# The second layer's modulation inside the first layer's channel mixing: VectorE multiply-adds on half slabs in a buffer of their own, in place of TensorE products on whole slabs

## The chip, the core and the metric

The kernel runs on one core of a Trainium2 chip. The metric is the device time of one execution in microseconds (us). TensorE is written PE (its weight loads PEld), VectorE DVE, ScalarE ACT, GpSimd POOL, and SyncE SP; SP issues every DMA that the text speaks of. All five take their instructions in order.

## The reference

A trunk of two layers over 512 latent tokens and 256 context tokens, 1024 channels, float32. What matters here, cut down:

```python
for i in range(DEPTH):                                   # DEPTH = 2
    mx = (silu_c @ w_ada[i] + b_ada[i])[:, None, :]      # latent:  (1024) @ (1024, 6144)
    mc = silu_cc @ w_ada[i] + b_ada[i]                   # context: the same weights
    sx1, ax1, gx1, sx2, ax2, gx2 = jnp.split(mx, 6, axis=-1)
    sc1, ac1, gc1, sc2, ac2, gc2 = jnp.split(mc, 6, axis=-1)
    ...
    x = x + gx1 * y_x
    x = x + gx2 * sqrelu_mlp(modulate(rmsnorm(x, norm2_g[i]), sx2, ax2), w_mlp1[i], w_mlp2[i])
    ...
def sqrelu_mlp(h, w1, w2):
    return jnp.square(jax.nn.relu(h @ w1)) @ w2          # 1024 -> 4096 -> 1024
```

Token mixing (convolution and attention) makes `y_x`; the context `h_ctx` goes the same way with `gc1`, `sc2`, `ac2` and `gc2`. The modulation `silu(c) @ w_ada[i]` has only two rows (latent and context), but reads 24 MB of weights per layer. It depends on no token, so layer 1's can be computed at any time before layer 1.

## The kernel before

**Layout and precision.** Channels lie on the 128 partitions, tokens in the columns: `X` is 128 x 8 x 768. Every large product keeps float32 precision in three matmuls: weights and activations are split into a high part (`whi`, `hh`, `fh`) and the remainder (`wlo`, `hl`, `fl`), and `mm3` (L102) adds high x high, high x low (L105) and low x high (L106). `fm_block` (L108) does this over the eight groups of 128 input channels: a block of 24 matmuls gives 128 output channels for one group of tokens, `LAT` (512) or `CTXS` (256).

**Weights.** `load_slab` (L84) loads 256 output columns (1 MB) into a raw buffer (tag `raw`; two of them in the channel mixing), ScalarE writes the high part in two halves (L76), and another engine the remainder (L77): VectorE, GpSimd, or one half on each (`both`). The split tiles have two buffers each in `wpool`.

**Channel mixing** (L1142 on). Four chunks `cch` of 1024 hidden channels. A chunk has two stages: four slabs of `w_mlp1`, whose blocks `f` end in `hidden` (L1144), and four slabs of `w_mlp2`, whose blocks `r` end in `residual` (L1079), which adds gate x product to `X` on VectorE. A slab has two blocks of 512 tokens (m = 0, 1), then two of 256. `hidden` does relu on ScalarE (`fr`), its square to the high part `fh` on ScalarE, the square in full precision on GpSimd in place (L1151), and the remainder `fl` on VectorE (L1152). A product lies in one of two PSUM banks for 512 tokens and one of two for 256 until relu or residual has read it. Chunk 0 of layer 0 and the second half of chunk 3 work in three groups of 256 tokens, since a norm stands ahead of the one and behind the other.

**Modulation.** `ada_slab` (L209) does 256 of the 6144 columns: a whole slab of `w_ada` (1 MB) into the same raw buffers, eight float32 products on TensorE with `cvec` (the two silu vectors) as the stationary side (L216), a copy on ScalarE (L222), two transposes on TensorE (L225) and small VectorE sums into `ad` (L228, L231). Layer 1's 24 slabs are done in layer 0's channel mixing: one behind each slab of `w_mlp1` (L1167) and one behind each slab of `w_mlp2` (L1192), so that chunks 0 to 2 hold them all.

**The norm** (`norm_mod`, L260) sums squares by matmuls with ones (`nc_n`), takes the power -1/2 on GpSimd (`ms_n`, L250), spreads it on VectorE over two diagonal tiles (`dg_n`, L253), broadcasts it by one matmul (`nb_n`, L257), and forms `nu_n`, `h2h` and `h2l` on VectorE, ScalarE and GpSimd.

**Order.** A scheduler in the framework orders each engine's instructions by a simulated timeline: program order where nothing is gained, earlier where the data are there earlier.

Of the kernel before, what the change touches and what calls it, by code (L numbers as in the profile page):

```python
# [51 lines left out]
def trunk_kernel(  # L52
# [156 lines left out]
    def ada_slab(i, L, s):  # L209
# [17 lines left out]
        for q in range(2):  # L227
# [6 lines left out]
            .to_broadcast([P, 2, 2]),  # L234
            op=ALU.add)

    def ada_gain(L, which, ks=slice(0, KT)):
# [149 lines left out]
    for i in range(DEPTH):  # L387
# [706 lines left out]

        def out_slabs(load, hidden, gate, nm, norm=None, after=None, ahead=()):
# [40 lines left out]
        if not last:  # L1136
            Ln = layer_params(i + 1)
            acc = xp.tile([P, NT], F32, tag="acc", name=f"acc{i}_3")
            ada_todo = list(range(24))
            hh = hpool.tile([P, KT, NT], F32R, tag="hh", name=f"h1h_{i + 1}")  # L1140
            hl = hpool.tile([P, KT, NT], F32R, tag="hl", name=f"h1l_{i + 1}")
        for cch in range(4):  # L1142
            fh, fl = [None] * KT, [None] * KT
            def hidden(w, mb, m, g):  # L1144
# [5 lines left out]
                nc.scalar.activation(out=fh[mb][:, g], in_=r[:, :W], func=AF.Square)  # L1150
                nc.gpsimd.tensor_tensor(out=r[:, :W], in0=r[:, :W], in1=r[:, :W], op=ALU.mult)  # L1151
                nc.vector.tensor_tensor(out=fl[mb][:, g], in0=r[:, :W], in1=f32(fh[mb][:, g]),  # L1152
# [5 lines left out]
            for s0 in ((0, 2), (2, 3), (3, 4)) if cch == 0 else ((n, n + 1) for n in range(4)):  # L1158
# [32 lines left out]
            def after(s):  # L1191
                if not last and ada_todo:  # L1192
                    ada_slab(i + 1, Ln, ada_todo.pop(0))
                if fin and not last:
                    nc.sync.dma_start(xs_d[i + 1][:, 2 * s : 2 * s + 2, :],
                                      X[:, 2 * s : 2 * s + 2, :])
                if fin and last:
# [15 lines left out]
                    w_mlp2[i][1024 * cch : 1024 * cch + 1024, 256 * s : 256 * s + 256]  # L1213
                    .rearrange("(k p) n -> p k n", p=P), f"w2_{i}_{cch}_{s}", lo_eng=None if last else both),
                lambda k: (fh[k], fl[k]), gate2, f"r{i}_{cch}",
                norm1 if fin and not last else None, after,
                (lambda: first.update(w=qk_slab(i + 1, 0, nc.gpsimd)),
                 lambda: first.update(v=v_slab(i + 1, 0, nc.gpsimd))) if fin and not last else ())
        if not last:
            while ada_todo:  # L1220
                ada_slab(i + 1, Ln, ada_todo.pop(0))
            state["ada_done"] = True
# [79 lines left out]
```

## Time and profile before

| | us |
|---|---|
| median of 3 runs | 2394.25 |
| lowest, highest run | 2392.32, 2401.45 |
| the profiled execution: its time | 2399.05 |
| the profiled execution: its span | 2397.3 |
| first `f` block of layer 0 starts at | 828.8 |
| first and last modulation products of layer 1 start near | 857.6, 1273 |
| granted TensorE clock, mean | 0.988 |

The profile is of one execution; times in it count from the start of the span. A row of the timeline gives start, duration, engine, line, operation, output<-input and shape; in brackets is the engine's idle time ahead of it and what ended that. Matmuls are pipelined, so the duration of one is longer than the step to the next. Names leave out buffer numbers: `r`, `f` and `adaps` are PSUM tiles, `r_w` a raw weight slab, `h_w` and `l_w` its two parts.

### The profile page before, as it was taken

The numbers are of one execution on the slowest core, as the hardware profiler recorded it, in microseconds if no ns is written. First come the engines' busy times: TensorE is split into PE (matmuls) and PEld (weight loads), VectorE is DVE, ScalarE is ACT, GpSimd is POOL, SyncE is SP. The second block draws the span as 40 slices with busy tenths as digits, with TensorE's granted clock in tenths as the row PEclk, the third lists the DMA queues.
The fourth block names the chain that finished last, engine by engine and source line by source line (L and its number), as shares of the span: only waits on it lengthen the run. The fifth ranks groups of instructions, "written<-read, shape, count | busy, mean of one in ns | idle before, by whom it ended". The sixth has DMA issues, their size and how long they took to land.

```text
span 2397.3 us, 36929 instructions
## 1 busy us (share of the span) xinstructions
PE 2317.9 (97%) x15034; PEld 2060.9 (86%) x15034; DVE 1349.1 (56%) x2311; ACT 928.7 (39%) x1837; POOL 679.7 (28%) x854
## 2 busy tenths in 40 slices
PE   7999999999999999999999998999999989999998
PEld 6999998888888988888888997999877879888887
DVE  6777776699556542222222356676759966433332
ACT  5555654522333342221312345555642323422331
POOL 2866754200000222120211256676620000200110
PEclk9999999999999999999999999999999999999999
DMA  8211111144535223333333221111123324232322
GB/s 292 66 43 37 45 45 42 45 158 139 163 113 176 71 89 106 124 123 106 124 114 98 78 64 54 45 43 41 47 73 132 117 72 134 82 100 90 103 90 69
DMA packets 222186, 224.79 MB, mean 94 GB/s; under 512 B 5872, under 2 KB 212160, under 8 KB 221888
## 3 DMA queue, kind: packets, MB, share of 16 engines
q1 hardware_dynamic: 222016, 222.43, 28.9%
q8 instruction: 118, 1.93, 0.3%
q14 instruction: 52, 0.43, 0.1%
HBM read 208.73 MB, written 13.67 MB: 93 GB/s over the span
## 4 chain that ended last, share of the span: by engine, by line
PE 86%; DVE 7%; ACT 3%; POOL 2%; DMA 1%; issue 1%; SPq 0%; ACTq 0%; POOLq 0%; DVEq 0%
PE r L104 6%; PE r L106 6%; PE f L104 6%; PE r L105 6%; PE f L105 6%; PE f L106 6%; PE gt L104 3%; PE gt L106 3%; PE gt L105 3%; PE qk L104 3%; PE qk L105 2%; PE qk L106 2%; PE adaps L216 2%; PE v L104 2%; PE yc L113 2%; PE v L106 2%
## 5 line engine op out<-in xcount | busy, mean ns | idle before, releaser
L104 PE MATMUL r<-fh,h_w 128*128 128x512 f32 (+1 forms) x832 | 285.8, 345 | 0.5 <-DVE X L1082 0.5
L104 PE MATMUL f<-h2h,h_w 128*128 128x512 f32 (+1 forms) x832 | 284.6, 345 | 1.3 <-ACT h2h L76 1.0
L105 PE MATMUL f<-h2l,h_w 128*128 128x512 f32 (+1 forms) x832 | 284.5, 343 | 1.1 <-POOL h2l L77 1.0
L105 PE MATMUL r<-fl,h_w 128*128 128x512 f32 (+1 forms) x832 | 283.5, 341 | 0.0
L106 PE MATMUL r<-fh,l_w 128*128 128x512 f32 (+1 forms) x832 | 283.5, 341 | 0.0
L106 PE MATMUL f<-h2h,l_w 128*128 128x512 f32 (+1 forms) x832 | 282.6, 342 | 0.0
L76 ACT ACTIVATE h_w<-r_w 128x1024 fp32r<-128x1024 f32 x128 | 128.7, 1052 | 312.1 <-PE r L105 131.0
L1151 POOL TENSOR_TENSOR fr<-fr 128x512 f32<-128x512 f32 (+1 forms) x104 | 93.1, 897 | 508.7 <-ACT fh L1150 508.7
L897 DVE SCALAR_TENSOR_TENSOR cacc<-z,cols,cacc 128x783 f32<-128x783 f32 (+1 forms) x240 | 201.2, 890 | 0.3
L104 PE MATMUL qk<-h_wqk,h1h 128*128 128x256 f32 x640 | 183.9, 289 | 5.3 <-ACT h1h L76 3.6
L1082 DVE SCALAR_TENSOR_TENSOR X<-r,ad,X 128x512 f32<-128x512 f32 (+1 forms) x104 | 64.9, 627 | 209.8 <-PE r L106 209.7
L105 PE MATMUL qk<-l_wqk,h1h 128*128 128x256 f32 x640 | 181.2, 285 | 0.0
L104 PEld LDWEIGHTS f<-h2h,h_w 128*128 128x128 f32 x832 | 157.6, 191 | 24.8 <-ACT fh L1150 2.5
L104 PEld LDWEIGHTS r<-fh,h_w 128*128 128x128 f32 x832 | 157.8, 190 | 23.6 <-issue 3.7
L106 PE MATMUL qk<-h_wqk,h1l 128*128 128x256 f32 x640 | 177.6, 285 | 0.0
L105 PEld LDWEIGHTS f<-h2l,h_w 128*128 128x128 f32 x832 | 158.4, 191 | 20.5 <-POOL h2l L77 2.5
L106 PEld LDWEIGHTS f<-h2h,l_w 128*128 128x128 f32 x832 | 158.3, 191 | 17.6
L664 DVE TENSOR_REDUCE st<-S 128x1 f32<-128x768 f32 (+1 forms) x160 | 134.7, 846 | 68.4 <-PE S L662 67.4
L106 PEld LDWEIGHTS r<-fh,l_w 128*128 128x128 f32 x832 | 157.8, 190 | 17.8
L105 PEld LDWEIGHTS r<-fl,h_w 128*128 128x128 f32 x832 | 158.0, 190 | 16.9
L77 DVE TENSOR_TENSOR l_w<-r_w,h_w 128x1024 fp32r<-128x1024 f32 x106 | 126.2, 1223 | 80.5 <-ACT h_w L76 78.9
L1152 DVE TENSOR_TENSOR fl<-fr,fh 128x512 fp32r<-128x512 f32 (+1 forms) x104 | 62.5, 605 | 189.4 <-POOL fr L1151 189.3
(247 smaller groups left out, 6257.1 us busy)
## 6 DMA issues: line engine op xcount, KB each, us to landing
r_w<-in_w_mlp_dram SPq DMA_DIRECT2D x64, 1024.0 KB, 5.4
ada<-in_w_ada_dram SPq DMA_DIRECT2D x48, 1024.0 KB, 5.2
r_wqk<-in_w_in_dram SPq DMA_DIRECT2D x32, 512.0 KB, 5.2
r_wg<-in_w_in_dram SPq DMA_DIRECT2D x16, 1024.0 KB, 5.2
r_wv<-in_w_in_dram SPq DMA_DIRECT2D x8, 1024.0 KB, 5.2
r_wao<-in_w_attn_out_dram SPq DMA_DIRECT2D x8, 1024.0 KB, 5.2
r_wo<-in_w_out_dram SPq DMA_DIRECT2D x8, 1024.0 KB, 8.2
at_d<-uo SPq DMA_DIRECT2D x40, 128.0 KB, 1.7
```

The costliest lines, as they stand in the source:

```text
L76: nc.scalar.activation(out=hi, in_=src, func=AF.Copy)
L77: (lo_eng or nc.vector).tensor_tensor(out=lo, in0=src, in1=f32(hi), op=ALU.subtract)
L104: nc.tensor.matmul(ps, sh, mh, start=first, stop=False)
L105: nc.tensor.matmul(ps, sh, ml, start=False, stop=False)
L106: nc.tensor.matmul(ps, sl, mh, start=False, stop=last)
L113: nc.tensor.matmul(ps, w[j][:, k, m0 : m0 + P], a(k)[0][:, toks], start=k + j == 0, stop=False)
L216: nc.tensor.matmul(ps[32 * j : 32 * j + 32, :256], cvec[:, k, :], r[:, k, :], start=k < 4, stop=k >= 4, tile_position=(0, 32 * j))
L664: nc.vector.tensor_reduce(out=st[:, m : m + 1], in_=S[:, :nkey], axis=AX.X, op=ALU.max, negate=True)
L897: nc.vector.scalar_tensor_tensor(out=ca[cc][:, :CV], in0=zt[cc][:, t : t + CV], scalar=wcol, in1=ca[cc][:, :CV], op0=ALU.mult, op1=ALU.add)
L1082: nc.vector.scalar_tensor_tensor(out=X[:, mb, g], in0=ps[:, :W], scalar=gate[:, s, mb : mb + 1], in1=X[:, mb, g], op0=ALU.mult, op1=ALU.add)
L1151: nc.gpsimd.tensor_tensor(out=r[:, :W], in0=r[:, :W], in1=r[:, :W], op=ALU.mult)
L1152: nc.vector.tensor_tensor(out=fl[mb][:, g], in0=r[:, :W], in1=f32(fh[mb][:, g]), op=ALU.subtract)
```

## The change

Layer 1's modulation in layer 0's channel mixing no longer uses TensorE for the product. A new generator `ada_rows` loads half a slab at a time (128 x 4 x 256, 512 KB) into a buffer `araw` of its own, of which there is one. For each of the four channel groups in the half and for each of the two rows it adds weights x a column of `cvec` into a tile `a` of 128 x 512: the first product of a slab by ScalarE, the others by VectorE's `scalar_tensor_tensor`. Then it starts the next half's load. Behind each second half, at the next step, four transposes and one reduction sum over the partitions. A step of the generator comes behind each block of 512 tokens (`tick`, `ada_step`), except the last of each `f` stage and the blocks in groups of 256: 3 + 8 steps in chunk 0, 15 in chunks 1 and 2, 7 in chunk 3, 48 in all; `drain` ends it ahead of the norm.

Two more things change. The remainders of all weight slabs in layer 0's channel mixing are made by GpSimd (before: VectorE, except three mlp1 slabs, and a half of each mlp2 slab). The full-precision square in `hidden` is made by ScalarE, in both layers.

```diff
+    def ada_rows(i, L):
+        def load(n):
+            r = state["rp"].tile([P, KT // 2, 256], F32, tag="araw", bufs=1, name=f"ar{i}_{n}")
+            nc.sync.dma_start(r, rows(w_ada[i], 256 * (n // 2), 256)[:, 4 * (n % 2) : 4 * (n % 2) + 4])
+            return r
+        r = load(0)
+        for n in range(48):
+            s = n // 2
+            if n % 2 == 0:
+                a = state["tp"].tile([P, 512], F32, tag="t2k", bufs=state["nt"], name=f"adaac{i}_{s}")
+                a = a.rearrange("p (q n) -> p q n", q=2)
+            for j in range(4):
+                k = 4 * (n % 2) + j
+                for q in range(2):
+                    if k == 0:
+                        nc.scalar.activation(out=a[:, q], in_=r[:, j], func=AF.Copy,
+                                             scale=cvec[:, k, q : q + 1])
+                    else:
+                        nc.vector.scalar_tensor_tensor(
+                            out=a[:, q], in0=r[:, j], scalar=cvec[:, k, q : q + 1], in1=a[:, q],
+                            op0=ALU.mult, op1=ALU.add)
+            if n < 47:
+                r = load(n + 1)
+            yield
+            if n % 2:
+                ps = state["mi"](f"adaps{i}_{s}")
+                for m in range(4):
+                    nc.tensor.transpose(ps[:, m * P : m * P + P],
+                                        a[:, m // 2, m % 2 * P : m % 2 * P + P], ident)
+                ad = L["ad"][:, :, 2 * s : 2 * s + 2]
+                nc.vector.tensor_reduce(out=ad, in_=ps.rearrange("p (q m k) -> p q m k", q=2, m=2),
+                                        axis=AX.X, op=ALU.add)
...
@@ out_slabs
                         out_block(w, s, g, m, hidden, gate, nm, norm)
+                        if tick and g is LAT:
+                            tick()
@@ mlp1_slab
-                                   f"w1_{i}_{cch}_{s}", lo_eng=nc.gpsimd if not last and cch + s < 2 else None)
+                                   f"w1_{i}_{cch}_{s}", lo_eng=None if last else nc.gpsimd)
@@ hidden
-                nc.gpsimd.tensor_tensor(out=r[:, :W], in0=r[:, :W], in1=r[:, :W], op=ALU.mult)
+                nc.scalar.activation(out=r[:, :W], in_=r[:, :W], func=AF.Square)
@@ the f stage
                             hidden(ws[s], 2 * s + m, m, g)
-                if not last and ada_todo:
-                    for _ in range(*s0):
-                        ada_slab(i + 1, Ln, ada_todo.pop(0))
+                            if g is LAT and (s, m) != (3, 1):
+                                ada_step()
             fin = cch == 3
             if fin and not last:
+                drain(ada_todo)
                 ada_gain(Ln, 0)
@@ after
-                if not last and ada_todo:
-                    ada_slab(i + 1, Ln, ada_todo.pop(0))
@@ the r stage
-                    .rearrange("(k p) n -> p k n", p=P), f"w2_{i}_{cch}_{s}", lo_eng=None if last else both),
+                    .rearrange("(k p) n -> p k n", p=P), f"w2_{i}_{cch}_{s}", lo_eng=None if last else nc.gpsimd),
-                norm1 if fin and not last else None, after,
+                norm1 if fin and not last else None, after, tick=ada_step, ahead=
```

How the order moves, at three places. The first is TensorE in the `r` stage of chunk 1 (names: `r_chunk_block_firsttoken`, the last number is a running one). Before, where the second slab's blocks begin:

```order
L104 MATMUL r_1_1_512_11286<-fh_1_7_10614,h_w_0_1_0_11202 128x256
L105 MATMUL r_1_1_512_11286<-fl_1_7_10615,h_w_0_1_0_11202 128x256
L106 MATMUL r_1_1_512_11286<-fh_1_7_10614,l_w_0_1_0_11203 128x256
L216 MATMUL adaps_12_11314<-ada_12_11312,cvec 32x256 x8
L104 MATMUL r_1_2_0_11338<-fh_1_0_10600,h_w_0_1_1_11332 128x512
L105 MATMUL r_1_2_0_11338<-fl_1_0_10601,h_w_0_1_1_11332 128x512
```

After, behind the first block of the same slab:

```order
L105 MATMUL r_1_2_0_11382<-fl_1_7_10627,h_w_0_1_1_11376 128x512
L106 MATMUL r_1_2_0_11382<-fh_1_7_10626,l_w_0_1_1_11377 128x512
L267 MATMUL adaps_9_11408<-cst,adaac_9_11275 128x128 x4
L104 MATMUL r_1_3_0_11426<-fh_1_0_10612,h_w_0_1_1_11376 128x512
L105 MATMUL r_1_3_0_11426<-fl_1_0_10613,h_w_0_1_1_11376 128x512
L106 MATMUL r_1_3_0_11426<-fh_1_0_10612,l_w_0_1_1_11377 128x512
```

The eight products between slabs are gone, and so are two transposes further on in the block; four transposes stand between the two blocks of 512 tokens.

The second is VectorE beside it: the residuals of this slab, before

```order
L228 TENSOR_REDUCE ad_9370<-adaps_12_11314 128x2 x2
L231 TENSOR_TENSOR ad_9370<-ad_9370,cols_9342 128x2x2
L77 TENSOR_TENSOR l_w_0_1_2_11463<-r_w_0_1_2_11460,h_w_0_1_2_11462 128x1024
L1082 SCALAR_TENSOR_TENSOR X_8446<-r_1_2_0_11338,ad_139,X_8446 128x512
L1082 SCALAR_TENSOR_TENSOR X_8446<-r_1_3_0_11364,ad_139,X_8446 128x512
L1082 SCALAR_TENSOR_TENSOR X_8446<-r_1_2_512_11390,ad_139,X_8446 128x256
L1082 SCALAR_TENSOR_TENSOR X_8446<-r_1_3_512_11416,ad_139,X_8446 128x256
```

and after (`ar_26`, `ar_27` are the halves of slab 13, `adaac_13` its sums):

```order
L1122 SCALAR_TENSOR_TENSOR X_8446<-r_1_2_0_11382,ad_139,X_8446 128x512
L270 TENSOR_REDUCE ad_9370<-adaps_9_11408 128x2x2
L258 SCALAR_TENSOR_TENSOR adaac_13_11855<-ar_26_11740,cvec,adaac_13_11855 128x256 x2
L272 TENSOR_TENSOR ad_9370<-ad_9370,cols_9342 128x2x2
L258 SCALAR_TENSOR_TENSOR adaac_13_11855<-ar_26_11740,cvec,adaac_13_11855 128x256 x4
L1122 SCALAR_TENSOR_TENSOR X_8446<-r_1_3_0_11426,ad_139,X_8446 128x512
L258 SCALAR_TENSOR_TENSOR adaac_13_11855<-ar_27_11864,cvec,adaac_13_11855 128x256 x6
L1122 SCALAR_TENSOR_TENSOR X_8446<-r_1_2_512_11462,ad_139,X_8446 128x256
L258 SCALAR_TENSOR_TENSOR adaac_13_11855<-ar_27_11864,cvec,adaac_13_11855 128x256 x2
L1122 SCALAR_TENSOR_TENSOR X_8446<-r_1_3_512_11488,ad_139,X_8446 128x256
```

Between the residuals of the slab now stand six multiply-adds of its first half and eight of its second, and each of the later residuals waits in line behind some of them.

The third is TensorE ahead of the first `f` blocks of the context tokens (512 on). Before:

```order
L106 MATMUL f_0_2_256_9572<-h2h_8456,l_w_0_0_1_9285 128x256
L257 MATMUL nb_n_0_512_9299<-dg_n_0_512_9296,cst 128x256
L157 MATMUL smps_9339<-cst,sm_9337 128x128 x2
L197 MATMUL lamps_9364<-lp_9344,cst 128x1
L104 MATMUL f_0_3_256_9602<-h2h_8456,h_w_0_0_1_9284 128x256
L105 MATMUL f_0_3_256_9602<-h2l_8457,h_w_0_0_1_9284 128x256
```

After:

```order
L106 MATMUL f_0_3_256_9605<-h2h_8456,l_w_0_0_1_9285 128x256
L297 MATMUL nb_n_0_512_9299<-dg_n_0_512_9296,cst 128x256
L157 MATMUL smps_9339<-cst,sm_9337 128x128 x2
L197 MATMUL lamps_9364<-lp_9344,cst 128x1
L267 MATMUL adaps_0_9944<-cst,adaac_0_9795 128x128 x4
L267 MATMUL adaps_1_10122<-cst,adaac_1_9951 128x128 x4
L104 MATMUL f_0_0_512_9635<-h2h_8456,h_w_0_0_0_9218 128x256
L104 MATMUL f_0_1_512_9665<-h2h_8456,h_w_0_0_0_9218 128x256
```

The block `f_0_3_256` moved ahead of the broadcast `nb_n_0_512`; behind the broadcast now come eight transposes and then at once the blocks that read its result.

More of the change, by code (lines that the diff above doesn't have):

```diff
@@ L235, in ada_slab @@
             op=ALU.add)
+    def ada_rows(i, L):
[30 more added lines that the diff above has]
+                                        axis=AX.X, op=ALU.add)
+                nc.vector.tensor_tensor(
+                    out=ad, in0=ad,
+                    in1=L["cols"][:, R_BADA + 2 * s : R_BADA + 2 * s + 2].unsqueeze(1)
+                    .to_broadcast([P, 2, 2]), op=ALU.add)
     def ada_gain(L, which, ks=slice(0, KT)):
@@ L1093, in out_block, with out_slabs @@
                 sumsq(acc, X, mb, g, f"s{nm}_{g.start}")
-        def out_slabs(load, hidden, gate, nm, norm=None, after=None, ahead=()):
+        def out_slabs(load, hidden, gate, nm, norm=None, after=None, ahead=(), tick=None):
             for s in range(2 if norm else 4):
@@ L1138, in trunk_kernel, with ada_step @@
             acc = xp.tile([P, NT], F32, tag="acc", name=f"acc{i}_3")
-            ada_todo = list(range(24))
+            rpool = tc.tile_pool(name="araw", bufs=1, reuse_waits="tile")
+            state["rp"] = rpool.__enter__()
+            ada_todo = ada_rows(i + 1, Ln)
             hh = hpool.tile([P, KT, NT], F32R, tag="hh", name=f"h1h_{i + 1}")
             hl = hpool.tile([P, KT, NT], F32R, tag="hl", name=f"h1l_{i + 1}")
+        def ada_step():
+            if not last:
+                next(ada_todo, None)
         for cch in range(4):
```

3 lines of the change are left out of this document (1 added, 2 removed).

## The prediction

> **What bounds the kernel now.** I read the engines' busy shares first, then the chain that ended last, then the busy time of the stretch that the change touches, the first layer's channel mixing.
>
> ```profile
> span 2397.3 us, 36929 instructions
> PE 2317.9 (97%) x15034; PEld 2060.9 (86%) x15034; DVE 1349.1 (56%) x2311; ACT 928.7 (39%) x1837; POOL 679.7 (28%) x854
> ...
> PE 86%; DVE 7%; ACT 3%; POOL 2%; DMA 1%; issue 1%; SPq 0%; ACTq 0%; POOLq 0%; DVEq 0%
> ```
>
> TensorE holds the chain, but shares over the whole span hide the stage. The busy time by stretch, for the stretch from the first `f` block to the end of the last `r` blocks (columns: stretch, its length, busy us of PE, PEld, DVE, ACT, POOL, granted clock, DMA share, GB/s):
>
> ```profile
> 828.00:1385.00 557.00, 555.16 (x3609) 483.53 (x3608) 166.89 (x298) 151.59 (x265) 114.02 (x99) 1.00 0.34 109
> ```
>
> TensorE is idle for under 2 of 557 us at full clock; VectorE is free for 390, GpSimd for 443. Work taken off TensorE here shortens the run until something else is late.
>
> **What one slab costs TensorE.** The timeline of TensorE around one of the 24 slabs, in start order; since matmuls overlap, I count from start to start.
>
> ```profile
> 910.26 1.07 PE L216 MATMUL adaps<-ada,cvec 128*32 128x256 f32 x16
> ...
> 928.06 0.28 PE L105 MATMUL r<-fl,h_w 128*128 128x256 f32 x1
> 928.18 0.28 PE L106 MATMUL r<-fh,l_w 128*128 128x256 f32 x1
> 928.39 1.07 PE L216 MATMUL adaps<-ada,cvec 128*32 128x256 f32 x16
> 929.39 0.50 PE L104 MATMUL r<-fh,h_w 128*128 128x512 f32 x1
> 929.73 0.40 PE L105 MATMUL r<-fl,h_w 128*128 128x512 f32 x1
> 929.96 0.39 PE L106 MATMUL r<-fh,l_w 128*128 128x512 f32 x1
> ...
> 934.05 0.40 PE L106 MATMUL r<-fh,l_w 128*128 128x512 f32 x1
> 934.29 0.38 PE L225 MATMUL adaps<-cst,adasb 128*128 128x128 f32 x2
> ...
> 934.74 0.39 PE L105 MATMUL r<-fl,h_w 128*128 128x512 f32 x1
> ```
>
> A 256-column matmul steps by 0.12 (928.06 to 928.18), a 512-column one by 0.23 (929.73 to 929.96). From 928.18 to 929.73 are 1.55 us, where 0.12 + 0.23 = 0.35 would do: the eight products cost **1.20**. From 934.05 to 934.74 are 0.69, where 2 x 0.23 would do: two transposes cost **0.23**. Both go.
>
> Four transposes come in their place. The nearest row is a group of four in the attention, in the same view:
>
> ```profile
> 298.99 0.28 PE L662 MATMUL S<-qk 128*128 128x256 f32 x1
> 299.11 0.60 PE L532 MATMUL qkT<-cst,dup 128*128 128x128 f32 x4
> 299.47 0.37 PE L104 MATMUL v<-h_wv,h1h 128*128 128x256 f32 x1
> 299.67 0.28 PE L105 MATMUL v<-l_wv,h1h 128*128 128x256 f32 x1
> ```
>
> 0.68 from 298.99 to 299.67, less 2 x 0.12: **0.44**. One slab saves 1.20 + 0.23 - 0.44 = 0.99, and 24 slabs **23.8 us**. Bounds: 23.0 if the group costs twice the pair (0.46) and 26 if it costs no more than 0.35.
>
> **What VectorE takes on.** 14 multiply-adds a slab (8 x 2, less two that ScalarE does), 336 in all, on 128x256 with both inputs in SBUF. The trace has no such row; beside it stand these, VectorE's timeline:
>
> ```profile
> 835.68 1.26 DVE L275 SCALAR_TENSOR_TENSOR nu_n<-X,A,nb_n 128x256 f32<-128x256 f32 x3 [0.85 <-PE nb_n L257]
> ...
> 567.77 7.64 DVE L897 SCALAR_TENSOR_TENSOR cacc<-z,cols,cacc 128x783 f32<-128x783 f32 x8
> ```
>
> Eight dependent ones of 783 columns step by 0.955, so 256 columns take at least a third, 0.31. Three of 256 in 1.26 are 0.42 each, which is the other end. I take 0.40, near the row of the same width: 134 us. Out go the `lo` halves that move to GpSimd (26 of mlp1, 16 of mlp2). The groups by line for 829 to 1440 have them, with what else changes engine (mean ns behind the comma):
>
> ```profile
> L77 DVE TENSOR_TENSOR l_w<-r_w,h_w 128x1024 fp32r<-128x1024 f32 x42 | 50.6, 1224 | 29.1 <-ACT h_w L76 29.1
> L77 POOL TENSOR_TENSOR l_w<-r_w,h_w 128x1024 fp32r<-128x1024 f32 x20 | 49.1, 2458 | 184.9 <-ACT h_w L76 184.9
> L1151 POOL TENSOR_TENSOR fr<-fr 128x512 f32<-128x512 f32 x28 | 29.7, 1062 | 171.3 <-ACT fh L1150 171.3
> L1150 ACT ACTIVATE fh<-fr 128x512 fp32r<-128x512 f32 x28 | 17.7, 632 | 0.9
> L1151 POOL TENSOR_TENSOR fr<-fr 128x256 f32<-128x256 f32 x40 | 27.0, 677 | 73.4 <-ACT fh L1150 73.4
> L1082 DVE SCALAR_TENSOR_TENSOR X<-r,ad,X 128x512 f32<-128x512 f32 x24 | 17.9, 748 | 34.1 <-PE r L106 34.1
> L1082 DVE SCALAR_TENSOR_TENSOR X<-r,ad,X 128x256 f32<-128x256 f32 x48 | 23.2, 483 | 75.3 <-PE r L106 75.2
> L222 ACT ACTIVATE adasb<-adaps 128x256 f32<-128x256 f32 x24 | 9.2, 382 | 123.9 <-PE adaps L216 122.0 <-PE adaps L225 2.0
> ```
>
> VectorE: 167 + 134 - 51 (42 x 1.22) = 250 of 533 us. GpSimd: 114 + 42 x 2.46 - 57 (its squares, 29.7 + 27.0) = 160. ScalarE: a square of 0.63 in place of GpSimd's 1.06, which makes the chain from `f` to `fl` shorter. None of the three is full; this work is hidden under TensorE. In the second layer only the square moves, and nothing there waits for it. What can go wrong is delay in order, not load.
>
> **The loop of the half slabs.** One buffer: the next half loads only when the last multiply-add of this half is done, so the time of two halves is a sum. For the load, 512 KB, the trace has no single one; the DMA issues give both sides:
>
> ```profile
> r_w<-in_w_mlp_dram SPq DMA_DIRECT2D x64, 1024.0 KB, 5.4
> ...
> at_d<-uo SPq DMA_DIRECT2D x40, 128.0 KB, 1.7
> ```
>
> Between them by size: 1.7 + 3.7 x 384/896 = 3.3. Two halves: 14 x 0.40 = 5.6, ScalarE's first products (two of 0.38) 0.8, residuals in between (of 0.75 and 0.48) about 0.9, two loads 6.6: **13.9 us**, 10.7 with loads of 1.7 and 18.1 with 5.4. A slab of TensorE lasts 18.1 now (910.26 to 928.39, from one product group to the next) and 17.1 after. So the loop fits. If it doesn't, VectorE's queue carries the delay to the `X` residuals behind the multiply-adds, and TensorE waits only when a residual is over 10.4 us late: the bank of a 512-token block is needed again after one block of 24 x 0.23 and two of 24 x 0.12, 11.2 us, less 0.75. Weights queue behind the half slabs on SP; they had shared two raw buffers with the modulation and now have both, one slab (17 us) earlier than needed. The transposes come three slabs behind their sums (in the order shown VectorE adds into `adaac_13` at the residual of `r_1_2`, where TensorE transposes `adaac_9`): no wait there.
>
> GpSimd's halves collide with the multiply-adds. One collision, GpSimd's and VectorE's timelines:
>
> ```profile
> 1377.49 2.44 POOL L77 TENSOR_TENSOR l_w<-r_w,h_w 128x1024 fp32r<-128x1024 f32 x1 [14.89 <-ACT h_w L76]
> ```
> ```profile
> 1377.70 2.52 DVE L294 TENSOR_TENSOR acc<-acc,nsq_sr 128x256 f32<-128x256 f32 x1
> ...
> 1381.16 0.43 DVE L294 TENSOR_TENSOR acc<-acc,nsq_sr 128x256 f32<-128x256 f32 x1 [0.54 <-ACT nsq_sr L293]
> ```
>
> An addition of 0.43 took 2.52 and ended just after GpSimd's half. A slab has two such halves: a loop that meets both is longer by 4.9. The halves of the next slab's weights run when a slab starts and its predecessor's buffer is free. Counted from the end of a slab's first 512-token block, where the loop begins, the odd half ends at 13.9 - 3.3 = 10.6 us and the next slab starts at 17.1 - 5.5 = 11.6, so I count none. The Trainium skill, "SBUF — State Buffer", Who interferes with whom, has this as a rule: VectorE with two SBUF inputs and a GpSimd instruction that reads SBUF exclude each other, and the second blocks until the first ends. The trace agrees (2.52 for 0.43); by that rule alone every multiply-add that meets a half waits, the third rival below.
>
> **The norm ahead of the first `f` blocks.** Two orders change here. Now the broadcast for tokens 256 to 511 is late:
>
> ```profile
> 830.03 4.71 POOL L77 TENSOR_TENSOR l_w<-r_w,h_w 128x1024 fp32r<-128x1024 f32 x2
> ```
> ```profile
> 830.09 4.73 DVE L253 TENSOR_SCALAR dg_n<-cst,ms_n 128x128 f32<-128x128 f32 x2 [0.87 <-POOL ms_n L250]
> ```
> ```profile
> 834.97 0.67 PE L257 MATMUL nb_n<-dg_n,cst 128*128 128x256 f32 x2 [1.83 <-DVE dg_n L253]
> ```
>
> ```profile
> 835.00:845.00 10.00, 10.00 (x70) 9.95 (x70) 7.87 (x16) 6.95 (x19) 4.45 (x7) 0.83 0.34 105
> ```
>
> TensorE waits 1.83, and its granted clock is 0.83 in the ten us after it, which is 1.7 us. In the new order `nb_n_0_256` stands some 48 matmuls later, so these 3.5 us go. But for the context tokens `nb_n_0_512` now stands behind `f_0_3_256`, and the products of two slabs that filled the time after it are gone:
>
> ```profile
> 853.64 0.43 PE nb_n L257 x2
> ```
> ```profile
> 861.65 0.48 DVE L283 SCALAR_TENSOR_TENSOR h2l<-nu_n,ad,h2h 128x256 fp32r<-128x256 f32 x1 [0.18 <-ACT h2h L279]
> ```
> ```profile
> L664 DVE TENSOR_REDUCE st<-S 128x1 f32<-128x768 f32 x128 | 121.2, 952 | 46.3 <-PE S L662 45.6
> ```
>
> From the broadcast to the last VectorE `h2l` are 8.5 us now, and six multiply-adds (2.4) and two reduces over a whole bank (0.6 each, 512/768 of the last row) now stand in between: 12. TensorE's own work in that time is two groups of four transposes (0.9), the small `smps` and `lamps` (0.6) and 48 x 0.12: 7.3. So it waits 1.2 (nothing in the way) to 4.8, and the clock may fall again, 1.7. I take 4.5 + 1.5 = 6, less the 3.5: **2.5 lost**, between a gain of 2.3 and a loss of 3.
>
> **Sum.** 23.8 - 2.5 = 21.3 us. The profiled execution took 2399.05 (1.75 around its span) and would take 2377.8; it lies 4.8 above the median of the three runs, 2394.25, from which I forecast **2373**.
>
> **Rivals.**
> 1. The forecast: by its bounds 26 + 2.3 to 23.0 - 3, so 2366 to 2374, and to 2380 with a few us of lateness in the loop. Chance 0.70.
> 2. Better still: GpSimd, free of its squares, shortens the waits where chunks meet (it now has an `fr` square of 1.06 in each chain from `f` to `r`); four such meetings of 1 us give 2362. Against it: TensorE is idle for only 1.8 of 557 us now. Chance 0.08.
> 3. The loop sets the pace. Both GpSimd halves always meet multiply-adds: 13.9 + 4.9 = 18.8, and with 15 of 16 blocks giving a step, 17.6 a slab against 17.1. Over some 22 slabs 11 us, the first 10 taken by the banks: 2374. With loads of 4.2 besides it is 20.6, or 19.3 a slab: 22 x 2.2 - 10 = 38, **2411**, slower. It decides above 19.8 for two halves, where the loss passes 21.3. For it: the 2.52 row, and weights of 1 MB on the same queues; against it: an overlap needs the odd half to be late already. Chance 0.10.
> 4. In between, the same loop near 19.3 for two halves (loads near 3.5 and both GpSimd halves, or 4.8 and one): 22 x (18.1 - 17.1) - 10 = 12, 2385 to 2390. Chance 0.12. That the products were off the path, and nothing changes, speaks the 555 of 557 us against.
>
> Half a per cent of 2394 is 12 us, about what a measurement of this kernel can tell from no change. So faster 0.78, same 0.12, slower 0.10. The range 2362 to 2392 takes in 1, 2 and 4 and leaves out the third.
>
> **What would show it.** Right: `adaps` rows of four transposes only after 830, slabs of 17.1 us, PE busy near 550 of 557 in the stage, TensorE's only new wait at `f` for `h2h`/`h2l` near 855 to 865, half-slab loads landing in 3.0 to 3.6, multiply-adds of 0.40 with few near 2.5. Wrong: waits of `r` or `f` matmuls for `X`, of `fr` for a bank, slabs growing towards the end of each `r` stage, or multiply-adds whose mean is over 0.6. If the transposes cost 0.7 in place of 0.44, 6 us of the gain go.

## The result and the profile after

| | before | changed |
|---|---|---|
| median, us | 2393.55 (4 runs, 2392.32 to 2401.45) | **2373.02** (4 runs, 2371.74 to 2380.49) |
| changed to before | | 0.9915, 95% interval 0.9898 to 0.9933 |
| the profiled execution: time, span | 2399.05, 2397.3 | 2371.74, 2370.0 |

The change takes 20.5 us off; 2373 had been forecast. The profile's page of the changed kernel (engines: busy us, share, instructions; then the shares of the chain that ended last):

```profile
span 2370.0 us, 36532 instructions
PE 2286.7 (96%) x14698; PEld 2050.6 (87%) x14698; DVE 1469.7 (62%) x2581; ACT 992.3 (42%) x1965; POOL 688.7 (29%) x792
...
PE 83%; DVE 8%; ACT 3%; POOL 3%; DMA 2%; issue 1%; SPq 0%; ACTq 0%; POOLq 0%; DVEq 0%
```

VectorE has 120 us more, TensorE 31 less. Where the time went is seen by cutting both executions at the same events: the first product of `o` (the projection ahead of the channel mixing), the first norm sum `nc_n`, the first `r`, and the first `r` of chunk 3. Busy time by stretch (columns as in the prediction), before:

```profile
758.49:809.97 51.48, 51.48 (x432) 51.48 (x431) 22.47 (x41) 13.41 (x24) 0.00 (x0) 1.00 0.38 123
809.97:911.26 101.29, 99.45 (x721) 89.15 (x719) 50.75 (x96) 44.70 (x97) 38.29 (x39) 0.98 0.26 84
911.26:1340.54 429.28, 429.28 (x2670) 367.89 (x2667) 107.18 (x197) 102.83 (x163) 75.64 (x62) 1.00 0.35 111
```

The same stretches, changed:

```profile
752.83:805.99 53.16, 53.16 (x446) 53.16 (x445) 33.32 (x70) 15.11 (x28) 0.00 (x0) 1.00 0.52 169
805.99:903.70 97.71, 92.50 (x650) 86.28 (x649) 61.55 (x127) 51.29 (x113) 36.70 (x25) 0.98 0.27 85
903.70:1313.00 409.30, 409.30 (x2391) 362.48 (x2389) 204.48 (x408) 138.15 (x235) 117.46 (x48) 1.00 0.34 110
```

From the first `r` to chunk 3's, 429.28 us have become 409.30, and TensorE is busy in every one of them: 20.0 of the gain. From there to the first `qk` of layer 1 both take 70.42. `o` begins at 758.49 before and 752.83 after, 5.7 us apart with the same work behind, which is scatter between two executions; it is why the two spans differ by 27.3 and the medians by 20.5. From `o` to the first `r` are 152.77 and 150.87: 1.9 gained, although TensorE is now idle for 5.2 us there (97.71 less 92.50) and was idle for 1.8; three slabs of products and the products of a fourth left it.

A measure that is free of that scatter is worth having: the time from the first `o` product to the first `r` of chunk 3, here **the stage**. Before it is 582.05, changed 560.17.

A group of four transposes in place (TensorE's timeline, changed kernel):

```profile
1061.56 0.40 PE L106 MATMUL r<-fh,l_w 128*128 128x512 f32 x1
1061.79 0.60 PE L267 MATMUL adaps<-cst,adaac 128*128 128x128 f32 x4
1062.15 0.48 PE L104 MATMUL r<-fh,h_w 128*128 128x512 f32 x1
1062.46 0.40 PE L105 MATMUL r<-fl,h_w 128*128 128x512 f32 x1
...
1078.92 0.60 PE L267 MATMUL adaps<-cst,adaac 128*128 128x128 f32 x4
```

From 1061.56 to 1062.46 are 0.90 where 2 x 0.23 would do: 0.44. The next group stands 17.13 later.

TensorE's waits behind the first norms (bracket: idle time and what ended it):

```profile
833.35 0.60 PE L297 MATMUL nb_n<-dg_n,cst 128*128 128x256 f32 x2
...
851.60 0.66 PE L267 MATMUL adaps<-cst,adaac 128*128 128x128 f32 x4 [0.58 <-DVE nlam L199]
854.25 0.39 PE L105 MATMUL f<-h2l,h_w 128*128 128x256 f32 x1 [1.75 <-DVE h2l L323]
857.75 0.50 PE L104 MATMUL f<-h2h,h_w 128*128 128x256 f32 x2 [1.29 <-ACT h2h L76]
858.73 0.39 PE L105 MATMUL f<-h2l,h_w 128*128 128x256 f32 x1 [0.49 <-POOL h2l L77]
```

The broadcast for tokens 256 to 511 (833.35) no longer waits; `f` waits for the context's `h2h` and `h2l`. What stands ahead of those on VectorE:

```profile
851.53 0.68 DVE L270 TENSOR_REDUCE ad<-adaps 128x4 f32<-128x512 f32 x1
852.13 0.87 DVE L258 SCALAR_TENSOR_TENSOR adaac<-ar,cvec,adaac 128x256 f32<-128x256 f32 x2
852.92 0.42 DVE L1201 TENSOR_TENSOR fl<-fr,fh 128x256 fp32r<-128x256 f32 x1
...
853.32 0.88 DVE L323 SCALAR_TENSOR_TENSOR h2l<-nu_n,ad,h2h 128x256 fp32r<-128x256 f32 x1
```

The multiply-adds as a group, from the page (busy us, mean ns, idle time ahead and its releaser), and one by one (ns: minimum, median, maximum):

```profile
L258 DVE SCALAR_TENSOR_TENSOR adaac<-ar,cvec,adaac 128x256 f32<-128x256 f32 x336 | 175.1, 574 | 81.9 <-DMA ar<-in_w_ada_dram 60.7
```
```profile
L258 DVE SCALAR_TENSOR_TENSOR adaac<-ar,cvec,adaac x336: 467/479/2621, 766.6 to 1253.3; 128x256 f32<-128x256 f32 x168
```

The median of 479 is a record's length; back to back they step by 0.40. The mean is 95 ns above the median, and the longest took 2.62 us. 20 of the 336 took over 1 us. The half-slab loads land after 3.3, 3.7 and 9.1 us (minimum, median, maximum).

### The profile page after: what moved, and what is told of

Same layout as the page of the kernel before. It is cut to its first block, busy times and chain, and to the rows that moved or that the text cites. A ratio compares the mean times of both kernels' runs of the same rounds, so it can differ in the third digit from the quotient of the medians.

```text
span 2370.0 us, 36532 instructions
## 1 busy us (share of the span) xinstructions
PE 2286.7 (96%) x14698; PEld 2050.6 (87%) x14698; DVE 1469.7 (62%) x2581; ACT 992.3 (42%) x1965; POOL 688.7 (29%) x792
## 4 chain that ended last, share of the span: by engine, by line
PE 83%; DVE 8%; ACT 3%; POOL 3%; DMA 2%; issue 1%; SPq 0%; ACTq 0%; POOLq 0%; DVEq 0%
PE r L104 6%; PE r L105 6%; PE r L106 6%; PE f L105 6%; PE f L104 6%; PE f L106 6%; PE gt L104 3%; PE gt L106 3%; PE gt L105 3%; PE qk L104 3%; PE qk L105 2%; PE qk L106 2%; PE v L104 2%; PE yc L113 2%; PE v L105 2%; PE v L106 2%
## 5 line engine op out<-in xcount | busy, mean ns | idle before, releaser
L77 POOL TENSOR_TENSOR l_w<-r_w,h_w 128x1024 fp32r<-128x1024 f32 x64 | 156.8, 2472 | 347.6 <-ACT h_w L76 347.6
L258 DVE SCALAR_TENSOR_TENSOR adaac<-ar,cvec,adaac 128x256 f32<-128x256 f32 x336 | 175.1, 574 | 81.9 <-DMA ar<-in_w_ada_dram 60.7
L707 ACT ACTIVATE e<-S,st 128x768 f32<-128x768 f32 (+1 forms) x160 | 130.8, 820 | 36.6 <-DVE st L704 36.5
```

The costliest lines, as they stand in the source:

```text
L77: (lo_eng or nc.vector).tensor_tensor(out=lo, in0=src, in1=f32(hi), op=ALU.subtract)
L258: nc.vector.scalar_tensor_tensor(out=a[:, q], in0=r[:, j], scalar=cvec[:, k, q : q + 1], in1=a[:, q], op0=ALU.mult, op1=ALU.add)
L707: nc.scalar.activation(out=e[:, :nkey], in_=S[:, :nkey], func=AF.Exp, bias=st[:, m : m + 1], accum_out=st[:, 2 + m : 3 + m])
```

## The experiments

Theory: the gain is TensorE's work alone, and everything that VectorE, ScalarE, GpSimd and the loads took on is hidden. Rivals: the engine moves bring part of it; or the loop of half slabs already costs something. Medians of different sessions are compared through before, which ran beside each; the stage is read from each profile.

| run | median, us | ratio to before, 95% | `o` to first `r` | first `r` to chunk 3's `r` | stage |
|---|---|---|---|---|---|
| before | | | 152.77 | 429.28 | 582.05 |
| changed | 2373.02 | 0.9898 to 0.9933 | 150.87 | 409.30 | 560.17 |
| e10, changed again | 2373.91 | 0.9892 to 0.9928 | 150.88 | 409.30 | 560.18 |
| e1, moves alone | 2397.39 | 0.9998 to 1.0019 | 153.23 | 429.27 | 582.50 |
| e2, without the moves | 2375.67 | 0.9910 to 0.9939 | 150.80 | 409.52 | 560.32 |
| e3, transposes twice | 2390.53 | 0.9967 to 0.9992 | 152.43 | 418.33 | 570.76 |
| e7, late start | 2402.14 | 1.0013 to 1.0037 | 144.89 | 443.93 | 588.82 |
| e4, two quarter buffers | 2382.57 | 0.9943 to 0.9975 | 149.14 | 418.54 | 567.68 |
| e8, late, two buffers | 2376.91 | 0.9916 to 0.9947 | 146.38 | 417.16 | 563.54 |
| e5, 4 more per half | 2428.33 | 1.0130 to 1.0168 | 147.63 | 457.90 | 605.53 |
| e6, 10 more per half | 2475.51 | 1.0325 to 1.0361 | 156.78 | 488.34 | 645.12 |
| e9, later start | 2379.28 | 0.9914 to 0.9947 | 144.42 | 420.16 | 564.58 |
| e11, GpSimd free | 2372.51 | 0.9878 to 0.9922 | 145.88 | 409.53 | 555.41 |
| **e12, e8 and e11** | **2364.98** | 0.9854 to 0.9896 | 142.50 | 410.17 | **552.67** |

**The changed kernel again (e10).**

> The changed kernel again, beside the others on one chip, so that a few us can be compared: 0.9915 of before, as measured, within 0.002.

0.9910; the stage is 560.18 against 560.17. So on these two executions the stage repeats to a hundredth of a microsecond, where the medians resolve about four. (A short stretch at half clock, which can come or stay away, is worth 1.7 of it; see the norm and the last section below.)

**The moves alone (e1).** On the kernel before:

```diff
-   f"w1_{i}_{cch}_{s}", lo_eng=nc.gpsimd if not last and cch + s < 2 else None)
+   f"w1_{i}_{cch}_{s}", lo_eng=None if last else nc.gpsimd)
...
-   nc.gpsimd.tensor_tensor(out=r[:, :W], in0=r[:, :W], in1=r[:, :W], op=ALU.mult)
+   nc.scalar.activation(out=r[:, :W], in_=r[:, :W], func=AF.Square)
...
-   lo_eng=None if last else both),
+   lo_eng=None if last else nc.gpsimd),
```

> The kernel before with the two engine moves alone: every weight remainder of layer 0's channel mixing on GpSimd, the square on ScalarE, the modulation still on TensorE in whole slabs. Theory (the gain is TensorE work taken away): TensorE issues the same matmuls, the steady stage stays at 18.1 us a slab, time within 3 us of before. Rival (the moves themselves free something): at least 10 us of the 20 appear here.

The stage is 0.45 us longer, the steady part the same to 0.01. The moves bring nothing by themselves.

**The changed kernel without the moves (e2).** The same diff turned round, on the changed kernel.

> The changed kernel with the two engine moves taken back: remainders as before (42 halves on VectorE), square on GpSimd, modulation as VectorE multiply-adds. Theory: VectorE has 51 us more in a stage of 544 where it is busy for 281, so TensorE still never waits: 20 us faster than before, within 4. By the collision reading the multiply-adds' mean falls from 574 ns towards 490 to 530, since GpSimd has 42 halves of 2.46 less and 68 squares of 1.06 and 0.68 more. Rival (the moves were needed to keep VectorE's loop in time): at least 6 us of the gain go, with waits of TensorE for X. Rival for the 574 ns (transfers into SBUF slow the multiply-adds): mean unchanged.

The stage is 560.32: the moves weren't needed either. The mean of the multiply-adds fell only to 548 ns, short of the 490 to 530 expected; GpSimd still has 68 squares and 20 remainder halves there, so this run doesn't decide what lengthens them. e11 does.

**Each group of transposes twice (e3).**

```diff
-                for m in range(4):
+                for m in (0, 1, 2, 3, 0, 1, 2, 3):
                     nc.tensor.transpose(ps[:, m * P : m * P + P],
```

> The changed kernel with each group of four transposes issued twice into the same bank. Theory: four transposes cost TensorE 0.39 to 0.44 in place, so 24 more groups cost 9 to 11 us against the changed kernel: 10 to 11 us faster than before are left, and an undisturbed slab lasts 17.5 in place of 17.1. Rival (the group hides in the weight loads beside it): under 3 us.

TensorE's timeline, two groups in the `r` stage of chunk 1:

```profile
1071.60 1.03 PE L267 MATMUL adaps<-cst,adaac 128*128 128x128 f32 x8
1089.15 1.03 PE L267 MATMUL adaps<-cst,adaac 128*128 128x128 f32 x8
```

17.55 from one to the next, 0.42 more than with four. The stage grew by 10.6, as the theory has it. The median lies 16.6 above e10's, and what the stage does not hold of that, 6 us less the scatter, stays open. In the profile it is not in the channel mixing: the 70.4 behind the stage are the same in e3.

**A late start (e7).** The first multiply-adds must wait for the last `h2h` of the context tokens:

```diff
+        cv = state["rp"].tile([P, KT, 2], F32, tag="cv2", bufs=1, name=f"cv2_{i}")
+        nc.vector.scalar_tensor_tensor(
+            out=cv, in0=late[:, :, 0:2], scalar=0.0, in1=cvec[:, :, 0:2],
+            op0=ALU.mult, op1=ALU.add)
...
-                                             scale=cvec[:, k, q : q + 1])
+                                             scale=cv[:, k, q : q + 1])
```

(`late` is `h2h` at token 512; the multiply-adds take `cv` likewise.)

> The changed kernel with the first multiply-adds made to depend on the last context h2h, through a copy of the two cvec columns. Theory: VectorE no longer has multiply-adds and reduces between the context broadcast and h2l, so of TensorE's 5.2 us of waits at 835 to 864 some 2 to 4 go and the loop catches up three slabs later at no cost: 2 to 4 us faster than the changed kernel, 22 to 25 faster than before. Rival (the transposes only filled a wait that is there anyway, the chain from broadcast to h2l): within 1 us of the changed kernel. Second rival: the three slabs come back as a wait at the end of layer 0: slower by 3 or more.

The second rival, worse than it said, and not at the end of layer 0. `o` to the first `r` fell by 6.0, so the multiply-adds in the norm do cost something. But then the loop, without the four halves done and the fifth loaded ahead, during `o`, ran against TensorE's order (TensorE's timeline):

```profile
912.00 0.79 PE L105 MATMUL r<-fl,h_w 128*128 128x512 f32 x1 [6.22 <-DVE fl L1205]
...
965.33 0.76 PE L104 MATMUL r<-fh,h_w 128*128 128x512 f32 x1 [3.41 <-DVE X L1126]
976.58 0.80 PE L104 MATMUL r<-fh,h_w 128*128 128x512 f32 x1 [3.92 <-DVE X L1126]
...
1211.13 0.80 PE L105 MATMUL r<-fl,h_w 128*128 128x512 f32 x1 [7.94 <-DVE fl L1205]
```

This is the prediction's third rival at work: `fl` and `X` stand in VectorE's queue behind multiply-adds that wait for their half or for GpSimd. Ahead of the first wait, five of them wait 3.32 for the load and then take 5.44 (from 905.90) beside two GpSimd halves (905.02 to 909.87). Over all 336 such collisions make 63 us here, where the changed kernel has 32.

**How near the edge is the loop? More multiply-adds (e5, e6).** Four, then ten more for each half, with a scalar of 0, so that the sums stay the same:

```diff
+            for j in range(4):
+                nc.vector.scalar_tensor_tensor(
+                    out=a[:, j % 2], in0=r[:, j % 4], scalar=0.0, in1=a[:, j % 2],
+                    op0=ALU.mult, op1=ALU.add)
             if n < 47:
                 r = load(n + 1)
```

> The changed kernel with four more multiply-adds (scalar 0, the sums unchanged) per half slab: 8 x 0.40 = 3.2 us more in the loop of two halves. Theory: in the trace of the changed kernel VectorE sits idle for the reduce or a residual for 5 us a slab in the r stages, so 12 us of loop and 3.2 more still fit under 17.1: within 3 us of the changed kernel. Rival (the loop is already the pace): 22 x 3.2 = 70 us slower.

> The changed kernel with ten more multiply-adds per half slab: 20 x 0.40 = 8 us more for two halves, 20 to 22.6 with one GpSimd half met. Theory by the prediction's third rival (it decides above 19.8): over the pace of 18.2 that the steps allow by 2 to 4 us a slab, so 15 to 80 us slower than the changed kernel, TensorE waiting for X and fl, although VectorE is busy for only some 430 of 544 us. Rival (only VectorE's sum counts): within 5 us.

For e5 the theory fell: the stage grew by 45.4 us (the median by some 55, of which the stage leaves 10 open). Most of the "5 us idle" that I had read is no room for more multiply-adds, as the changed kernel's own trace shows. SyncE's issue of a half slab, one slab apart, ScalarE's first products, and VectorE:

```profile
1056.34 0.37 SPq L242 DMA_DIRECT2D ar<-in_w_ada_dram  x1
```
```profile
1073.24 0.37 SPq L242 DMA_DIRECT2D ar<-in_w_ada_dram  x1
```
```profile
1062.43 0.91 ACT L255 ACTIVATE adaac<-ar,cvec 128x256 f32<-128x256 f32 x2 [3.98 <-PE adaps L267]
```
```profile
1052.66 2.47 DVE L258 SCALAR_TENSOR_TENSOR adaac<-ar,cvec,adaac 128x256 f32<-128x256 f32 x6 [1.15 <-DMA ar<-in_w_ada_dram]
1055.05 0.48 DVE L1122 SCALAR_TENSOR_TENSOR X<-r,ad,X 128x256 f32<-128x256 f32 x1
1055.44 0.87 DVE L258 SCALAR_TENSOR_TENSOR adaac<-ar,cvec,adaac 128x256 f32<-128x256 f32 x2
1056.52 0.48 DVE L1122 SCALAR_TENSOR_TENSOR X<-r,ad,X 128x256 f32<-128x256 f32 x1 [0.20 <-PE r L106]
1061.99 0.75 DVE L1122 SCALAR_TENSOR_TENSOR X<-r,ad,X 128x512 f32<-128x512 f32 x1 [4.99 <-PE r L106]
1062.66 0.68 DVE L270 TENSOR_REDUCE ad<-adaps 128x4 f32<-128x512 f32 x1
1063.26 0.87 DVE L258 SCALAR_TENSOR_TENSOR adaac<-ar,cvec,adaac 128x256 f32<-128x256 f32 x2
```

The last multiply-add of a half ends at 1056.3 and the next half's load is issued at 1056.34. It lands 3.74 later, at 1060.08: that much of VectorE's 4.99 us of idle the loop needs anyway. ScalarE's two first products start only at 1062.43, behind the transposes at 1061.79; the bracket names the transposes, and I take it that the buffer of the sums comes free there. So here a load that lands up to 2.35 later changes nothing, and the `X` residual and the reduce run meanwhile. At the second half there is no such room: VectorE waits 0.91 for the load at 1069.56. Of the 16.9 us from issue to issue the loop thus needs 14.6, with 2.3 of slack, in a slab without a collision.

In e5 the loop runs free of TensorE, issue to issue 20.6 (1096.98 to 1117.62):

```profile
1100.65 4.13 DVE L258 SCALAR_TENSOR_TENSOR adaac<-ar,cvec,adaac 128x256 f32<-128x256 f32 x2 [3.08 <-DMA ar<-in_w_ada_dram]
...
1109.86 0.67 DVE L274 TENSOR_REDUCE ad<-adaps 128x4 f32<-128x512 f32 x1
1113.66 0.89 DVE L258 SCALAR_TENSOR_TENSOR adaac<-ar,cvec,adaac 128x256 f32<-128x256 f32 x2 [3.13 <-ACT adaac L255]
```
```profile
1099.56 4.93 POOL L77 TENSOR_TENSOR l_w<-r_w,h_w 128x1024 fp32r<-128x1024 f32 x2 [12.50 <-ACT h_w L76]
```
```profile
1096.98 12.69 SPq L242 DMA_DIRECT2D ar<-in_w_ada_dram  x2
...
1117.62 0.37 SPq L242 DMA_DIRECT2D ar<-in_w_ada_dram  x1
```

Two multiply-adds of 0.40 took 4.13, and ended just after GpSimd's two halves (1104.49): a collision of 3.3. The padding is 8 x 0.40 = 3.2. Without both the loop is 20.6 - 3.3 - 3.2 = 14.1. So e5's loss is padding and collisions together. Over 17 slabs of e5 (918.26 to 1270.70) the mean from issue to issue is 20.7, 2.4 of it collisions; without them 18.3 would be left, which is what 15 steps in 16 blocks of 17.1 allow. By that estimate the padding alone would have cost about nothing; no run here pads the kernel with GpSimd free.

The prediction's own formula, 22 x (20.6 x 15/16 - 17.1) - 10, gives 39; measured are 45. e6 is 85 us longer in the stage (the median by some 102), over the 15 to 80 expected, and another 8 behind it (78.6 us to the first `qk` of layer 1 in place of 70.4), while VectorE is busy for only 317 of 425 us (905 to 1330): the sum of VectorE's work does not decide, the loop does.

**Loads beside multiply-adds (e4).** The same 4 KB as two buffers of a quarter slab:

```diff
-            r = state["rp"].tile([P, KT // 2, 256], F32, tag="araw", bufs=1, name=f"ar{i}_{n}")
-            nc.sync.dma_start(r, rows(w_ada[i], 256 * (n // 2), 256)[:, 4 * (n % 2) : 4 * (n % 2) + 4])
+            r = state["rp"].tile([P, 2, 256], F32, tag="araw", bufs=2, name=f"ar{i}_{n}")
+            nc.sync.dma_start(r, rows(w_ada[i], 256 * (n // 4), 256)[:, 2 * (n % 4) : 2 * (n % 4) + 2])
...
+                if n < 47 and j % 2:
+                    rq[j // 2] = load(2 * n + 2 + j // 2)
```

> The changed kernel with the same 4 KB of buffer cut into two quarter-slab buffers of 256 KB loads, so that a load runs beside the multiply-adds of the other quarter. Theory (the loop of load and multiply-adds hides under TensorE's slab, which sets its pace through the reduce that waits for the transposes): within 3 us of the changed kernel, 19 to 23 faster than before, the steady stage still 68.6 us for four slabs. Rival (the serial loads already cost something): over 4 us faster than the changed kernel.

Neither: 7.5 us slower in the stage, by one wait and the clock behind it (9.2, less 1.7 gained ahead of the first `r`). From chunk 1 on it takes the same 341.8 us to chunk 3's `r` as the changed kernel, as the theory says; but in the first `r` stage five multiply-adds met GpSimd's two halves (911.33 to 916.37) with an `fl` behind them (VectorE, then TensorE):

```profile
910.41 6.24 DVE L258 SCALAR_TENSOR_TENSOR adaac<-ar,cvec,adaac 128x256 f32<-128x256 f32 x5 [2.57 <-DMA ar<-in_w_ada_dram]
916.58 0.68 DVE L1201 TENSOR_TENSOR fl<-fr,fh 128x512 fp32r<-128x512 f32 x1
```
```profile
917.31 0.80 PE L105 MATMUL r<-fl,h_w 128*128 128x512 f32 x1 [6.94 <-DVE fl L1201]
```

**Late start and two buffers (e8).** Both diffs.

> The late start of the run before (first multiply-adds behind the last context h2h) together with the two quarter buffers. Theory (the late start lost because load and multiply-adds in series could not catch up with the order, 23 us of TensorE's waits for X and fl and 12 us of clock behind them): with loads beside multiply-adds those waits go, and what the late start saves in the norm stage stays: 2365 to 2373, the fastest yet. Rival (too many multiply-adds ahead of fl and X in VectorE's queue, whatever the loads): waits of 3 to 8 us stay, over 2390.

In between. Of e7's 23 us of waits one of 4.17 is left, at 913.24, for an `fl` that stood behind seven multiply-adds waiting for a load; the stage is 25 us shorter than e7's, so series loading was what e7 lost by. Of the 6.0 us that e7 saved in the norm 4.5 are kept (the same wait of 1.83 at the broadcast is followed by half clock here and was not in e7), but the one wait and its clock take 7.9.

**A still later start (e9).** As e8, but `late` is the last `fl` of 512 tokens in chunk 0, and

```diff
-                            if g is LAT and (s, m) != (3, 1):
+                            if g is LAT and cch > 0:
                                 ada_step()
```

> The two quarter buffers, with the first multiply-adds behind the last 512-token fl of chunk 0 (not only the context h2h) and the steps of chunk 0's first stage moved to the ends of the later first stages, so that no multiply-add stands ahead of an fl in VectorE's queue before the products of chunk 0 begin. Theory: the norm stage keeps what the late start saved (146.4 us from the first output product to the first r against 150.9 in the changed kernel), and the wait of 4.2 us for fl with its 3.4 us of clock goes: 560.2 - 4.5 = 556 us from the first output product to the last r stage, 2367 to 2370, 3 to 6 faster than the changed kernel. Rival (the burst that catches up now stands ahead of the X residuals of the first r stage): 5 to 15 us of waits there, 2375 or more.

The rival: the burst moved ahead of the `X` residuals. VectorE and GpSimd there:

```profile
962.24 5.10 DVE L262 SCALAR_TENSOR_TENSOR adaac<-ar,cv,adaac 128x256 f32<-128x256 f32 x2
967.26 0.47 DVE L1126 SCALAR_TENSOR_TENSOR X<-r,ad,X 128x256 f32<-128x256 f32 x1
```
```profile
962.03 5.02 POOL L77 TENSOR_TENSOR l_w<-r_w,h_w 128x1024 fp32r<-128x1024 f32 x2 [21.05 <-ACT h_w L76]
```

Two multiply-adds last as long as GpSimd's two halves (5.10 against 5.02), and TensorE waits 2.91 for the `X` behind them (at 967.79).

**GpSimd free (e11).** The changed kernel with every remainder of layer 0's channel mixing on VectorE (`lo_eng=None` in both places).

> The changed kernel with every weight remainder of layer 0's channel mixing on VectorE, squares on ScalarE, so that GpSimd has nothing to do beside the multiply-adds once the norms are done. Collision theory: none of the multiply-adds is over 1 us, and their mean falls from 574 ns to the median's 480. The loop of two halves gets two remainders of 1.22 more and loses some 1.3 of collisions; since four padded multiply-adds per half already cost 55 us, it is at the edge: 0 to 25 us slower than the changed kernel. Rival (transfers into SBUF or the reads of TensorE slow them): mean over 540 as before.

```profile
L258 DVE SCALAR_TENSOR_TENSOR adaac<-ar,cvec,adaac 128x256 f32<-128x256 f32 x336 | 144.1, 480 | 39.6 <-DMA ar<-in_w_ada_dram 29.1
```
```profile
L258 DVE SCALAR_TENSOR_TENSOR adaac<-ar,cvec,adaac x336: 469/479/643, 773.4 to 1253.2; 128x256 f32<-128x256 f32 x168
```

The mean is the median, 480, and the longest 643 ns. The loop is not at the edge: the remainders, 2 x 1.22 us a slab, fall into the time in which VectorE waits for a load, and the steady part is as long as in the changed kernel to 0.2. The stage is even 4.8 us shorter, all of it ahead of the first `r`, where TensorE is idle for 1.9 us in place of 5.2. The median cannot be told from the changed kernel's.

**The late start, two buffers, and GpSimd free (e12).**

> The late start with two quarter buffers, and every remainder on VectorE so that GpSimd no longer blocks multiply-adds. Theory (the 4.2 us wait for fl in the late start came from multiply-adds that a GpSimd half had held up): from the first output product to the first r 144.5 to 146.5, no wait over 1 us after that, 553 to 556 from the first output product to the last r stage against 560.2 in the changed kernel and 555.4 with remainders on VectorE alone: 2366 to 2370. Rival (with the catch-up burst in one queue with the remainders, l_w comes late): waits of TensorE for l_w or fl of 3 us or more near 880 to 930, 2373 or more.

```profile
755.07:897.57 142.50, 141.87 (x1085) 136.76 (x1083) 87.41 (x185) 67.81 (x143) 12.24 (x15) 1.00 0.35 111
897.57:1307.74 410.17, 410.17 (x2398) 363.25 (x2397) 240.79 (x481) 137.50 (x233) 0.00 (x0) 1.00 0.36 113
```

TensorE is idle for 0.6 us in 553, at full clock throughout: better than expected in all three figures. e8's wait for `fl` is gone; there two multiply-adds at 892.16 and 893.90 had taken 4.4 beside GpSimd's halves. 2364.98 is 8.0 us below the changed kernel, with an interval (0.9854 to 0.9896) that ends below the 0.9910 and 0.9915 of its two sessions but overlaps theirs; the stage, 7.5 us shorter, is the firmer evidence. It is the fastest of the kernels.

## Why the prediction came out

1. **TensorE's work** (23.8 us forecast). Right. Four slabs took 72.45 with the products (chunk 1's `r` stage before, 1056.18 to 1128.63), take 68.58 with the transposes (1039.16 to 1107.74) and 67.00 in chunk 3's `f` stage before (1273.54 to 1340.54), which has no products and one last pair of transposes: 66.77 without that pair's 0.23. So 1.42 a slab went and 0.45 came, where I had 1.43 and 0.44 from single rows. Net 0.97 against 0.99. e3 finds 0.41 for a group by doubling it.
2. **The other engines' work is hidden.** Right as a result: TensorE is busy in all of 409.30 us. e1 and e2 show that the engine moves neither bring nor save anything. VectorE's 281 of 544 us (829 to 1373; 250 of 533 forecast) have 32 us of collisions in them, (574 - 480) x 336.
3. **The half-slab loop** (13.9 of 17.1 us forecast). It fits, and the loop by itself was sized right: 14.1 in e5 without padding and collision, 14.6 by the slack of 2.3 in the changed kernel. Its terms were off both ways: loads land after 3.7 and not 3.3 (0.8 for two), but the residual of 512 tokens, which I had counted, and the reduce, which I had not, run while ScalarE and the load are waited for. "I count none" was wrong for the collisions: 32 us in 24 slabs, some 1.3 a slab, and nearly twice that in e5 and e7; multiply-adds near 2.5 us were not few. That the forecast held all the same was in part luck: it was owed to the halves done ahead, during `o`, which the prediction does not count on; e7, without them, lost the whole gain. The break-even that the third rival named, 19.8 for two halves, fits e5; its chance of 0.10 was too small for a loop with 2.3 of slack and collisions of 3.3.
4. **The norm** (2.5 lost forecast). The mechanism was right: the wait of 1.83 at the broadcast is gone, and `f` waits behind 854 for the context's `h2h` and `h2l`. TensorE is idle for 5.2 us in all, and one stretch at half clock follows (0.57 over 859 to 863) as one did before (0.66 over 835 to 839): 6.9 with its 1.7, where 6 were forecast. The stage gained 21.9 where 24 x 0.97 = 23.3 would be, so 1.4 was lost net. That is less than the 2.5 because the old order had hidden a cost that I had not counted: its products behind the norm stood scattered among the `f` products (TensorE's timeline before):

```profile
857.38 0.28 PE L106 MATMUL f<-h2h,l_w 128*128 128x256 f32 x1
857.59 0.62 PE L216 MATMUL adaps<-ada,cvec 128*32 128x256 f32 x2
858.14 0.38 PE L104 MATMUL f<-h2h,h_w 128*128 128x256 f32 x1
```

   One product (two records) takes 0.76 - 0.12 = 0.64. The sixteen of two slabs, up to 863.97 among 21 `f` products, cost 6.59 - 21 x 0.12 = 4.1, where the forecast's 2 x 1.20 is 2.4. These 1.7 make up for the longer waits, and that the norm's term came so near is luck.
5. **Sum**: 20.0 + 1.9 = 21.9 in the two profiles against 21.3 forecast, 20.5 by the medians. That the median met the forecast to the microsecond is luck too, since medians here resolve about four.

The Trainium skill's rule that I weighed ("SBUF — State Buffer", Who interferes with whom: a VectorE instruction with two SBUF inputs and a GpSimd instruction that reads SBUF exclude each other for the whole instruction) agrees with e11's 643 ns maximum against 2621 and with e9's pair. I had quoted it and then counted no collision, because I placed the halves by an average schedule.

## What to carry to other kernels

Work moved onto an idle engine is bounded by the loop it stands in (load, first product, and whatever waits ahead in the same queue), not by that engine's busy share; idle time that is the loop's own load is no slack for the loop, though other work can fall into it (e11). A few extra instructions in the loop show in one run whether there is room, and the trace then has to say what filled it: in e5 collisions did so nearly as much as the padding. In a loop that meets such collisions any reordering can cost more than the change brought (e4, e7). Free the loop first (loads beside work, no GpSimd operation on SBUF beside two-input VectorE work), and only then move it.

## What was not expected of the hardware

- One float32 product alone among `f` products cost TensorE 0.64 us (the rows above), three in a row 0.65 (860.00 in the kernel before), eight in a row 1.20: the first costs most.
- The half clock came after short waits, but not after each. In the kernel before, 1.83 us of idle were followed by a granted clock of 0.83 over ten us (the prediction's rows); e8's same wait of 1.83 was followed by 0.66 over four us, and e11's of 1.38 by 0.69 over four. In e1, e7 and e9 the same wait of 1.83 or 1.84 was followed by full clock, and in e12, with no wait over 0.31, the clock was full throughout. The Trainium skill, "TensorE: Matmul & The Clock Gate", Part 1, has the half clock after an idle window of about 3.4 us; here a wait of about half of that could bring it, and what decides whether it does was not measured. In e5, with 34.7 us of waits between 905 and 1330, the clock there was 0.97, some 12 us more by an estimate (0.03 of 425).
- Loads of 256 KB land after 2.8 us (median in e4 and e8), of 512 KB after 3.7, of 1 MB after 5.5: halving a load saves 1.8 and 0.9 us, not half.
